# A decoder block on one core: low parts of the attention scores as pairs of 64-row products

## The chip, the core and the metric

The kernel runs on one core of a Trainium2 chip. The core has a matrix engine (TensorE, PE in the profile) that multiplies operands held in the on-chip memory SBUF and writes sums to PSUM, eight banks of 512 float32 in each of 128 partitions. VectorE (DVE), ScalarE (ACT) and GpSimd (POOL) do the elementwise work; SyncE (SP) issues most transfers between SBUF and device memory. Each engine works through its own queue in order, and semaphores hold an instruction until what it needs is done. The metric is the device time of one execution in microseconds. Before the change three runs took 1271.04, 1269.61 and 1268.10 us; the median is 1269.61.

## What is computed

One layer of a decoder block in float32, sequence 1024, width 1024. A normalised input goes through one combined projection; its parts feed a pooling mixer, a causal differential attention with four heads, and two gates. The gated sum goes through an output projection, and a gated feed-forward net follows. The change touches the attention, cut here to what matters:

```python
def block(args):
    qa, qb, start = args
    dist = (start + jnp.arange(Q_BLOCK))[:, None] - kpos[None, :]
    causal = dist >= 0
    bias = -slopes[:, None, None] * dist.astype(jnp.float32)[None]

    def probs(qq, kk):
        s = jnp.einsum('bhqd,bhkd->bhqk', qq, kk).astype(jnp.float32) * scale + bias
        s = jnp.where(causal, s, -jnp.inf)
        return jax.nn.softmax(s, axis=-1)

    a = probs(qa, k1) - lam * probs(qb, k2)
    return jnp.einsum('bhqk,bhkd->bhqd', a.astype(vh.dtype), vh)
```

Each head has two maps of scores, one from each pair of 64-wide queries and keys, and attends with the difference of their softmaxes.

## The kernel before

**Precision.** TensorE's float32r products keep fewer bits than float32. So each operand is split into a high part (the value cast to float32r) and a low part (the rest, cast too), and a product of two operands is made as three: high by high, high by low, low by high. `triple` (lines 231 to 235) issues them.

**Stages.** The queries, keys, values and gates come from a Strassen-like scheme of seven products (`seven_steps`, lines 258 to 283): each step is four triples, and the sums lie in PSUM tiles named Y, Z and X. A unit of seven steps makes two blocks of 128 output columns; the weights are converted just ahead (`weights`, `weight_operand`). The split queries and keys of a head go to device memory in `qkd` (line 292), as 128 partitions by 2 parts (high, low) by 1024 positions, with map 0 in partitions 0 to 63 and map 1 in 64 to 127. Then comes the attention, and after it the second branch, the output projection and the feed-forward net.

**Loading a head.** `load_head` (line 632) makes three operands for the scores. In `K[:, m]`, the high part of map m's keys lies in that map's 64 partitions (`hs[m]`) and its low part in the other 64. `QA[:, m]` has the high part of the queries in both halves, and `QB[:, m]` the low part in both halves. One product over 128 rows with QA is therefore high by high plus high by low, and one with QB is low by high plus low by low. `QB` is loaded by four transfers of 64 partitions. For head 0 the function is resumed in two places: QA and K are loaded before the fourth pair of gates (line 652), QB and V after the first step of the last gate unit (line 658). Heads 1 to 3 are loaded while an earlier head is worked on (lines 843 and 894).

**Scores.** `scores` (line 731) makes one row of 128 queries of one head. The row sees 128 times (qb + 1) keys; up to 512 are one block (nj = 1), more are two equal blocks (nj = 2). For each map it takes a PSUM tile of two banks (`pair`, two such tiles in all), issues the products with QA and QB for each block, and reduces on DVE: line 754 adds the distance term `negd` and finds the extreme, and line 757 takes the exponential on ACT. `transposes` and `values` follow for earlier rows. X of a running unit and the transposed heads take their PSUM tile from the same two.

**Order.** `step` (line 875) walks these generators and, by the costs that they yield (PE and DVE work in microseconds, from `map_cost` and the like), puts products of a filler between them: the rest of the last gate unit and the first branch's projection. What comes out is not yet the queue. Outside the parts under a manual schedule, a scheduler orders the instructions of every engine anew, by readiness in its own model and by free buffers, and the semaphores hold at run time. So products that stand together in a loop can stand apart in TensorE's queue.

**Buffers.** SBUF tiles of 8 KB a partition come from 16 slots (`a8`), those of 4 KB from 14 (`b4`). The slots of 4 KB also hold the converted weights (Wh, Wl), the score rows E, their transposes AT, the outputs O, the distances `negd` and the loaded gates.

Of the kernel before, what the change touches and what calls it, by code (L numbers as in the profile page):

```python
# [11 lines left out]
F32R = mybir.dt.float32r  # L12
# [3 lines left out]
P = 128  # L16
S = 1024
# [24 lines left out]
def block_kernel(ctx, tc, x, w_in, pool_mix, pool_scale, w_branch_a, lam_q1, lam_k1, lam_q2,  # L42
                 lam_k2, subln_g, w_branch_b, w_out, mix_pre_g, mix_post_g, ffn_pre_g, ffn_post_g,
                 w_ffn_gate, w_ffn_up, w_ffn_down, out):
    nc = tc.nc
    x, out = x[0], out[0]
# [16 lines left out]
    def name(s):  # L63
        uid[0] += 1
        return f"{s}_{uid[0]}"

    def a8(shape, dt, s):
        return sb.tile(shape, dt, tag="a8", bufs=A8, name=name(s))

    def b4(shape, dt, s):  # L70
        return sb.tile(shape, dt, tag="b4", bufs=B4, name=name(s))
# [7 lines left out]
    def pair(s):  # L79
        return ps.tile([P, 2, HALF], F32, tag="pair", bufs=2, name=name(s))  # L80

    def small(n, s):
        return sm.tile([P, n], F32, tag="small", bufs=20, name=name(s))

    def f32(ap):
        return ap.bitcast(F32)
# [205 lines left out]
    qkd = [[dr.tile([P, 2, S], F32, name=name("qkd")) for _ in range(2)] for _ in range(NH)]  # L292
# [318 lines left out]
    for i in range(2):  # L611
        nc.vector.tensor_tensor_reduce(out=lamt[:, 4, :], in0=lamt[:, 2 * i, :], in1=lamt[:, 2 * i + 1, :],
                                       scale=1.0, scalar=0.0, op0=ALU.mult, op1=ALU.add,
# [16 lines left out]
    hs = [slice(0, HD), slice(HD, P)]  # L630

    def load_head(h):

        QA, K = (a8([P, 2, S], F32R, n) for n in ("QA", "K"))
        for m in range(2):
            r, r2 = hs[m], hs[1 - m]
            nc.sync.dma_start(f32(K[r, m, :]), qkd[h][1][r, 0, :])
            nc.sync.dma_start(f32(K[r2, m, :]), qkd[h][1][r, 1, :])
            for rr in (r, r2):
                nc.sync.dma_start(f32(QA[rr, m, :]), qkd[h][0][r, 0, :])  # L640
        yield
        QB, V = (a8([P, 2, S], F32R, n) for n in ("QB", "V"))
        for m in range(2):
            for rr in hs:
                nc.sync.dma_start(f32(QB[rr, m, :]), qkd[h][0][hs[m], 1, :])
        nc.sync.dma_start(f32(V), vd[h])
        heads[h] = QA, QB, K, V.rearrange("p i (b d) -> p b i d", b=NB)

    head0 = load_head(0)
    for i, pair_cols in enumerate(gate_pairs[:-1]):  # L650
        if i == 3:
# [59 lines left out]
        nc.scalar.copy(ma[t][d // 4][:, d % 4, :], o)  # L711


    def map_cost(qb):
        return 0.227 * (qb + 1), 0.23 + 0.136 * (qb + 1)

    def combine_cost(qb):
        return 0.0, 0.55 + 0.136 * (qb + 1)

    def turn_cost(n):  # L720
        return 0.109 * n, 0.15 + 0.136 * n

    def value_cost(n, last):
        return 0.24 * n, 0.35 if last else 0.0

    def row_cost(qb):
        n = qb + 1
        turns = [turn_cost(min(4, n - b)) for b in range(0, n, 4)]
        return [sum(c) for c in zip(map_cost(qb), map_cost(qb), combine_cost(qb), *turns, value_cost(n, True))]

    def scores(h, qb):

        QA, QB, K, V = heads[h]
        slope = 0.25 ** (h + 1)
        L = P * (qb + 1)
        nj = 1 if L <= HALF else 2
        w = L // nj
        q = slice(qb * P, (qb + 1) * P)
        if nj == 1:
            E = b4([P, 2, HALF], F32, "E")  # L740
            E = [E[:, 0, :L], E[:, 1, :L]]
        else:
            E = [b4([P, S], F32, "E")[:, :L] for _ in range(2)]
        nm, sums = small(2, "nm"), small(2, "sums")
        dv = negd[:, S - L:S].rearrange("p (j w) -> p j w", j=nj)
        for m in range(2):
            sc = pair("s")
            for j in range(nj):
                c = slice(j * w, (j + 1) * w)
                nc.tensor.matmul(sc[:, j, :w], QA[:, m, q], K[:, m, c], start=True, stop=False)  # L750
                nc.tensor.matmul(sc[:, j, :w], QB[:, m, q], K[:, m, c], start=False, stop=True)
            e = E[m].rearrange("p (j w) -> p j w", j=nj)

            nc.vector.tensor_tensor_reduce(out=e, in0=sc[:, :nj, :w], in1=dv, scale=-slope,
                                           scalar=3.0e38, op0=ALU.add, op1=ALU.min,
                                           accum_out=nm[:, m:m + 1])
            nc.scalar.activation(E[m], E[m], AF.Exp, bias=nm[:, m:m + 1], scale=-1.0,
                                 accum_out=sums[:, m:m + 1])
            yield map_cost(qb)
        rec, cf = small(2, "rec"), small(1, "cf")  # L760
        nc.vector.reciprocal(rec, sums)
        nc.vector.tensor_scalar(cf, sums[:, 0:1], rec[:, 1:2], nlam, op0=ALU.mult, op1=ALU.mult)
        nc.vector.scalar_tensor_tensor(out=E[0], in0=E[1], scalar=cf, in1=E[0], op0=ALU.mult, op1=ALU.add)
        attends[h, qb] = E[0], rec
        yield combine_cost(qb)
# [67 lines left out]
    def filling():  # L833
        yield from last_unit
        for i in range(2):
            y2.append((a8([P, 2, S], F32R, "y2h"), a8([P, 2, S], F32R, "y2l")))
            for j in range(2):
                for t, s in zip(y2[i], range(2)):
                    nc.sync.dma_start(f32(t[:, j, :]), yd[2 * i + j][:, s, :])
        ma.extend([[a8([P, 4, HALF], F32, "ma") for _ in range(KD // 4)] for _ in range(2)])  # L840
        first = branch(0, w_branch_a, quad_mov(y2), take_a)
        next(first)
        for _ in load_head(1):
            pass
        yield from first
        next(second)
# [11 lines left out]
    AHEAD = 4  # L858
    steps, late = 0, []
    whole = [sum(c) for c in zip(*(row_cost(qb) for _, qb in seq))]  # L860
    whole[0] += FILLING * (24 + 4 * 2 * KD)
    done = [0.0, 0.0]
# [26 lines left out]
    for i in range(-AHEAD, len(seq)):  # L889
        j = i + AHEAD  # L890
        if j < len(seq):
            h, pos = divmod(j, len(QORDER))
            if pos == 2 and 0 < h < NH - 1:
                for _ in load_head(h + 1):
                    pass
            step(scores(*seq[j]))
        j = i + 1
        if 0 <= j < len(seq):
            step(transposes(*seq[j]))
        if i >= 0:  # L900
            step(values(*seq[i]))
            h, pos = divmod(i, len(QORDER))
            if h < NH - 1 and pos == len(QORDER) - 1:
                head_norm(h)
            elif h == NH - 1 and pos < NH - 1:
                for t in range(2):
                    turn_head(pos, t)
            elif h == NH - 1 and pos % 4 == 3:
                b = slice(4, 8) if pos == 3 else slice(0, 4)
                head_norm(h, b)  # L910
                defer(LAG, partial(turn_head, h, b.start // 4))
# [365 lines left out]
    for n, (i, kb) in enumerate(stream):  # L1277
        fetch(n + DEPTH + 3)
        if n + DEPTH < len(stream):
            j, kj = stream[n + DEPTH]  # L1280
# [52 lines left out]
```

## Time and profile before

| | |
|---|---|
| median of three runs | 1269.61 us |
| span of the profiled execution | 1265.6 us |
| lowest and highest run | 1268.10, 1271.04 us |
| mean granted TensorE clock | 0.998 |
| first and last start of a score product | 327.2 and 481.1 us |
| score products with QA, with QB | 96, 96 |
| transposes of the score rows (line 778), products with V (line 792) | 144, 288 |

The profile is of one execution; the span runs from its first to its last instruction. A line of groups names the source line, the engine, the operation, the tiles (out<-in), the shapes and the count, then the busy time, the mean duration in nanoseconds and the idle time ahead with what ended it. PEld is the weight load of a product, which can run under the product before it. In the timeline the first column is the start and the second the duration in microseconds; the ends of products are modelled, and they overlap. A line of windows gives the stretch and its length, then busy time and count of PE, PEld, DVE, ACT and POOL (of PE and PEld alone, where only these have work on the chosen line), the granted clock, the share of the DMA engines and GB/s. A line of waits says who waited for whom: total, times and longest, in microseconds. SPq is SyncE's queue of transfers.

### The profile page before, as it was taken

What the parts mean: (1) busy time and instruction counts of PE and PEld (TensorE: products, weight loads), DVE (VectorE), ACT (ScalarE), POOL (GpSimd) and SP (SyncE); (2) the same over time, 40 slices, a digit from 0 to 9 for tenths busy, and PEclk for the clock granted to TensorE, in tenths of its full rate; (3) what the DMA queues carried; (4) which work ended last, traced back from release to release, by engine and by line L of the source; (5) the groups of instructions that cost most, each with busy time, mean ns of one, the idle gap of its engine ahead of it and who ended that gap; (6) DMA issues with size and microseconds to landing.
All of it is one profiled execution on the core that took longest, in us unless ns stands there. A gap on an engine that the chain in (4) does not pass through costs nothing.

```text
span 1265.6 us, 15699 instructions
## 1 busy us (share of the span) xinstructions
PE 1246.5 (98%) x5912; PEld 1039.1 (82%) x5912; DVE 838.6 (66%) x1296; ACT 582.7 (46%) x1042; POOL 142.7 (11%) x128
## 2 busy tenths in 40 slices
PE   8999999999999999999999999999999999999997
PEld 7888888888788887888888888888888888888886
DVE  5985784534578888855697655655656547955666
ACT  7553344434477774444553333333333333554542
POOL 4100000000201100000102111011111011000221
PEclk9999999999999999999999999999999999999999
DMA  7354338323797108533314322323322368733236
GB/s 253 114 189 132 135 128 243 115 85 117 259 250 206 34 18 283 169 115 134 117 45 139 125 100 89 103 100 108 125 99 84 125 215 279 238 95 105 87 96 208
DMA packets 135452, 179.15 MB, mean 142 GB/s; under 512 B 7632, under 2 KB 90320, under 8 KB 132944
## 3 DMA queue, kind: packets, MB, share of 16 engines
q1 hardware_dynamic: 124544, 146.56, 37.0%
q10 hardware_dynamic: 10832, 31.59, 6.5%
q8 instruction: 46, 0.75, 0.3%
q14 instruction: 30, 0.25, 0.1%
HBM read 124.39 MB, written 53.74 MB: 141 GB/s over the span
## 4 chain that ended last, share of the span: by engine, by line
PE 89%; DVE 3%; ACT 2%; DMA 2%; issue 2%; POOL 1%; SPq 0%; POOLq 0%; DVEq 0%; ACTq 0%
PE Y L235 10%; PE Y L234 10%; PE Y L233 10%; PE X L235 5%; PE X L234 5%; PE X L233 5%; PE Z L235 3%; PE Z L234 3%; PE Z L233 3%; PE Yd L234 3%; PE Yd L235 3%; PE Yd L233 3%; PE o L792 2%; PE branch L233 2%; PE branch L235 2%; PE branch L234 2%
## 5 line engine op out<-in xcount | busy, mean ns | idle before, releaser
L162 DVE TENSOR_TENSOR p<-Z,p 128x512 f32<-128x512 f32 x35 | 24.2, 691 | 163.3 <-PE Z L235 160.7
L234 PE MATMUL Y<-A_lo,Wh 128*128 128x512 f32 x296 | 115.5, 390 | 0.3 <-DVE A_lo L89 0.3
L233 PE MATMUL Y<-A_hi,Wh 128*128 128x512 f32 x296 | 115.2, 389 | 0.0
L235 PE MATMUL Y<-A_hi,Wl 128*128 128x512 f32 x296 | 115.2, 389 | 0.0
L233 PE MATMUL Y<-S_hi,Wh 128*128 128x512 f32 x280 | 109.2, 390 | 0.0
L233 PE MATMUL X<-S_hi,Wh 128*128 128x512 f32 x280 | 109.2, 390 | 0.0
L235 PE MATMUL Y<-S_hi,Wl 128*128 128x512 f32 x280 | 109.1, 390 | 0.0
L234 PE MATMUL Y<-S_lo,Wh 128*128 128x512 f32 x280 | 109.1, 390 | 0.0
L235 PE MATMUL X<-S_hi,Wl 128*128 128x512 f32 x280 | 108.9, 389 | 0.0
L234 PE MATMUL X<-S_lo,Wh 128*128 128x512 f32 x280 | 108.9, 389 | 0.0
L202 ACT CAST Wh<-wf_t 128x1024 fp32r<-128x1024 f32 x70 | 72.8, 1053 | 72.1 <-PE X L234 30.6
L202 ACT CAST Wh<-w_raw 128x1024 fp32r<-128x1024 f32 x72 | 60.6, 843 | 66.7 <-PE Z L234 40.0
L89 DVE TENSOR_TENSOR w_op<-wd,w_op 128x512 fp32r<-128x512 f32 x77 | 56.1, 729 | 52.8 <-ACT w_op L166 52.6
L89 DVE TENSOR_TENSOR Wl<-wf_t,Wh 128x1024 fp32r<-128x1024 f32 x70 | 86.6, 1245 | 4.8 <-ACT Wh L202 4.8
L166 ACT CAST w_op<-wd 128x512 fp32r<-128x512 f32 x77 | 47.9, 622 | 78.1 <-PE Yd L235 31.4
L89 DVE TENSOR_TENSOR Wl<-w_raw,Wh 128x1024 fp32r<-128x1024 f32 x72 | 70.4, 977 | 14.5 <-ACT Wh L202 14.5
L233 PE MATMUL Yd<-w_op,s_op 128*128 128x512 f32 x176 | 68.7, 390 | 0.6 <-ACT w_op L166 0.6
L234 PE MATMUL Yd<-w_op,s_op 128*128 128x512 f32 x176 | 68.7, 390 | 0.3 <-DVE w_op L89 0.3
L235 PE MATMUL Yd<-w_op,s_op 128*128 128x512 f32 x176 | 68.3, 389 | 0.0
L162 DVE TENSOR_TENSOR wf_t<-w_raw,wf_t 128x512 f32<-128x512 f32 x70 | 65.7, 938 | 1.1
L234 PEld LDWEIGHTS Y<-A_lo,Wh 128*128 128x128 f32 x296 | 55.6, 188 | 12.1 <-DVE A_lo L89 0.7
L233 PEld LDWEIGHTS Y<-A_hi,Wh 128*128 128x128 f32 x296 | 55.6, 188 | 11.6
(269 smaller groups left out, 3058.7 us busy)
## 6 DMA issues: line engine op xcount, KB each, us to landing
s_raw<-fsd SPq DMA_DIRECT2D x35, 512.0 KB, 3.6
w_raw<-in_w_in_dram SPq DMA_DIRECT2D x32, 512.0 KB, 4.3
w_raw<-in_w_ffn_gate_dram SPq DMA_DIRECT2D x22, 512.0 KB, 3.8
w_raw<-in_w_ffn_up_dram SPq DMA_DIRECT2D x22, 512.0 KB, 3.8
fsd<-fss SPq DMA_DIRECT2D x11, 1024.0 KB, 3.9
wd<-in_w_ffn_down_dram SPq DMA_DIRECT2D x44, 256.0 KB, 5.4
fsd<-F SPq DMA_DIRECT2D x33, 256.0 KB, 2.3
qkd<-qk_st ACTq DMA_DIRECT2D x16, 512.0 KB, 3.8
```

The lines of the kernel that those rows point to most:

```text
L89: nc.vector.tensor_tensor(out=o, in0=a, in1=f32(hi), op=ALU.subtract)
L162: nc.vector.tensor_tensor(out=o, in0=a, in1=b, op=op)
L166: nc.scalar.copy(hi, a)
L202: nc.scalar.copy(hi, a)
L233: nc.tensor.matmul(o, ah, bh, start=start, stop=False, skip_group_check=goes_on)
L234: nc.tensor.matmul(o, ah, bl, start=False, stop=False, skip_group_check=goes_on)
L235: nc.tensor.matmul(o, al, bh, start=False, stop=stop, skip_group_check=goes_on)
L792: nc.tensor.matmul(o, ats[b // 4][:, j, b % 4 * P:(b % 4 + 1) * P], V[:, b, :, :], start=b == 0 and j == 0, stop=b == qb and j == 1)
```

## The change

`QB` becomes one tile of 4 KB that holds the low part of the queries as it lies in device memory, map 0 in partitions 0 to 63 and map 1 in 64 to 127, and is loaded by one transfer, ahead of the point where `load_head` is left for the first time. `scores` takes the PSUM tiles of both maps at once and issues the products with QA for map 0, then for map 1. Then, block by block, it issues for each map a product over the 64 partitions of that map, on `QB[hs[m]]` and the high part of the keys. The built program marks these with a division of the array into 64 rows by 128 columns, at row 0 for map 0 and at row 64 for map 1. The term low by low is no longer computed. The reductions follow after all products of both maps. The planner's costs change with it: the PE cost of a row's two maps, twice 0.227 for each block of 128 keys, becomes 0.34, all put down to the first.

```diff
@@ load_head
+        QB = b4([P, S], F32R, "QB")
+        nc.sync.dma_start(f32(QB), qkd[h][0][:, 1, :])
         yield
-        QB, V = (a8([P, 2, S], F32R, n) for n in ("QB", "V"))
-        for m in range(2):
-            for rr in hs:
-                nc.sync.dma_start(f32(QB[rr, m, :]), qkd[h][0][hs[m], 1, :])
+        V = a8([P, 2, S], F32R, "V")
         nc.sync.dma_start(f32(V), vd[h])
@@ costs
-    def map_cost(qb):
-        return 0.227 * (qb + 1), 0.23 + 0.136 * (qb + 1)
+    def map_cost(qb, m):
+        return (0.34 * (qb + 1), 0.0)[m], 0.23 + 0.136 * (qb + 1)
...
@@ scores
+        sc = [pair("s") for _ in range(2)]
         for m in range(2):
-            sc = pair("s")
             for j in range(nj):
-                c = slice(j * w, (j + 1) * w)
-                nc.tensor.matmul(sc[:, j, :w], QA[:, m, q], K[:, m, c], start=True, stop=False)
-                nc.tensor.matmul(sc[:, j, :w], QB[:, m, q], K[:, m, c], start=False, stop=True)
+                nc.tensor.matmul(sc[m][:, j, :w], QA[:, m, q], K[:, m, j * w:(j + 1) * w], start=True, stop=False)
+        for j in range(nj):
+            for m in range(2):
+                nc.tensor.matmul(sc[m][:, j, :w], QB[hs[m], q], K[hs[m], m, j * w:(j + 1) * w],
+                                 start=False, stop=True)
+        for m in range(2):
             e = E[m].rearrange("p (j w) -> p j w", j=nj)
 
-            nc.vector.tensor_tensor_reduce(out=e, in0=sc[:, :nj, :w], in1=dv, scale=-slope,
+            nc.vector.tensor_tensor_reduce(out=e, in0=sc[m][:, :nj, :w], in1=dv, scale=-slope,
                                            scalar=3.0e38, op0=ALU.add, op1=ALU.min,
                                            accum_out=nm[:, m:m + 1])
             nc.scalar.activation(E[m], E[m], AF.Exp, bias=nm[:, m:m + 1], scale=-1.0,
                                  accum_out=sums[:, m:m + 1])
-            yield map_cost(qb)
+            yield map_cost(qb, m)
```

In the changed program the products with QA stand on line 748 and those with QB on line 751.

More of the change, by code (lines that the diff above doesn't have):

```diff
@@ L728, in row_cost @@
         turns = [turn_cost(min(4, n - b)) for b in range(0, n, 4)]
-        return [sum(c) for c in zip(map_cost(qb), map_cost(qb), combine_cost(qb), *turns, value_cost(n, True))]
+        return [sum(c) for c in zip(map_cost(qb, 0), map_cost(qb, 1), combine_cost(qb), *turns, value_cost(n, True))]
     def scores(h, qb):
```

## The prediction

> **What bounds the kernel now.** I read the page first (busy time, chain of waits), then the windows of the stage that the change touches, then that stage's waits, then single products in the timeline.
>
> ```profile
> span 1265.6 us, 15699 instructions
> PE 1246.5 (98%) x5912; PEld 1039.1 (82%) x5912; DVE 838.6 (66%) x1296; ACT 582.7 (46%) x1042; POOL 142.7 (11%) x128
> ...
> PE 89%; DVE 3%; ACT 2%; DMA 2%; issue 2%; POOL 1%; SPq 0%; POOLq 0%; DVEq 0%; ACTq 0%
> ```
>
> TensorE is busy for 98% of the span and carries 89% of the chain that ended last. The scores run from 327 to 481 us. The windows give the whole stage (span, then PE, weight loads, DVE, ACT, POOL), and the products of lines 751 and 750 alone:
>
> ```profile
> 325.00:482.00 157.00, 154.07 (x910) 132.28 (x908) 124.90 (x311) 111.11 (x289) 17.36 (x9) 1.00 0.53 158
> ...
> 325.00:482.00 157.00, 32.75 (x96) 18.11 (x96) 1.00 0.53 158
> ...
> 325.00:482.00 157.00, 33.65 (x96) 18.09 (x96) 1.00 0.53 158
> ```
>
> Here, too, TensorE has 3 us of idle time in 157, and its clock is granted in full (1.00). DVE at 125 us and ACT at 111 us leave room. So what is added to TensorE's queue lengthens the kernel, and what is taken out shortens it. TensorE's waits in this stage are few:
>
> ```profile
> PE s L751 <- DMA QB<-qkd: 1.9, 1, 1.9
> PE oT L826 <- DVE O L811: 1.2, 1, 1.2
> PE o L792 <- DVE O L798: 0.8, 2, 0.6
> PE s L750 <- DVE nm L754: 0.7, 3, 0.3
> ```
>
> What one product costs is read from starts that follow each other, since the durations overlap (column 1 is the start, column 2 the duration):
>
> ```profile
> 440.05 0.39 PE L751 MATMUL s<-K,QB 128*128 128x512 f32 x1
> 440.28 0.39 PE L750 MATMUL s<-K,QA 128*128 128x512 f32 x1
> ...
> 446.19 0.36 PE L751 MATMUL s<-K,QB 128*128 128x448 f32 x1
> 446.39 0.36 PE L750 MATMUL s<-K,QA 128*128 128x448 f32 x1
> ...
> 450.41 0.35 PE L751 MATMUL s<-K,QB 128*128 128x384 f32 x1
> 450.59 0.34 PE L750 MATMUL s<-K,QA 128*128 128x384 f32 x1
> ```
>
> A low product takes 0.23 us at 512 columns, 0.20 at 448 and 0.18 at 384. It is recorded for 0.39 us, so 0.16 us of it is still in flight while the next product streams.
>
> **The change, part by part.** *The low products themselves.* The 96 low products stay 96, over the same columns; each now uses 64 rows of the array in place of 128. One that stands alone streams the same columns and saves nothing. Time falls only where a product in rows 0 to 63 is followed directly by one in rows 64 to 127, so that both stream at once. Whether it is depends on the order of TensorE's queue, which the scheduler makes and not the loops. In the built program it is this for the third and fourth row of queries ("..." stands for products of the running unit and transposes):
>
> ```
> L748 Matmult s_2830<-K_2143,QA_2142 128x448 x2
> L751 Matmult s_2830<-K_2143,QB_2152 128x448 x2
> ...
> L748 Matmult s_2831<-K_2143,QA_2142 128x448 x2
> L751 Matmult s_2831<-K_2143,QB_2152 128x448 x2
> ...
> L748 Matmult s_2863<-K_2143,QA_2142 128x256
> L751 Matmult s_2863<-K_2143,QB_2152 128x256
> ...
> L748 Matmult s_2864<-K_2143,QA_2142 128x256
> L751 Matmult s_2864<-K_2143,QB_2152 128x256
> ```
>
> The second map's products come later, with other work between; I take the reason to be its score buffer, which comes free later. I counted through the whole queue: the 96 low products stand in 66 groups, and only 9 of the 48 possible pairs are neighbours, 3 of 512 columns, 2 of 448 and 4 of 384. If these overlap fully they save 3 x 0.23 + 2 x 0.20 + 4 x 0.18 = 1.8 us; if not, nothing. I take 1.8.
>
> *The switches.* Each of the 66 groups is entered from a product over all 128 rows and left to one: 132 changes between the whole array and half of it. The trace of before has no 64-row product, so the price has to be bounded. From below: nothing. Products of other lines, shapes and buffers follow each other at the same 0.23 us now, and a change of rows could be just as free. For the upper end, two things that are hidden now could be laid open. One is the 0.16 us in flight, if the array must be empty before its division changes. The other is the weight load:
>
> ```profile
> 334.47 0.47 PE L751 MATMUL s<-K,QB 128*128 128x512 f32 x1 [1.85 <-DMA QB<-qkd]
> 334.78 0.40 PE L750 MATMUL s<-K,QA 128*128 128x512 f32 x1
> 335.01 0.39 PE L751 MATMUL s<-K,QB 128*128 128x512 f32 x1
> ...
> 334.55 0.19 PEld L750 LDWEIGHTS s<-K,QA 128*128 128x128 f32 x1
> 334.78 0.19 PEld L751 LDWEIGHTS s<-K,QB 128*128 128x128 f32 x1
> ...
> 448.99 0.71 PE L778 MATMUL aT<-ident,E 128*128 128x128 f32 x5
> 449.45 0.48 PE L233 MATMUL branch<-y2h,wb_hi 128*128 128x512 f32 x1
> 449.77 0.39 PE L234 MATMUL branch<-y2l,wb_hi 128*128 128x512 f32 x1
> ```
>
> In the steady run a load (0.19 us) starts with the product before it (334.78 beside 334.78) and costs nothing. Where it could not, after the wait at 334.47 and after the short transposes at 448.99, the next start comes 0.31 and 0.32 us later in place of 0.23: an uncovered load costs 0.09. So a switch lies between 0 and 0.16 + 0.09 = 0.25 us, and 132 of them between 0 and 33 us. The two nearest rows are the uncovered load (0.09) and the tail (0.16); I know of no row that tells which one a switch lays open, and take their middle, 0.125 us: 16.5 us. TensorE has no idle time near the groups that would hide it.
>
> The Trainium skill, in "TensorEngine Tiling (Array Packing)", Key Properties, says that changing the tiling mode drains TensorE, whereas a change of tile within one mode does not. The 0.39 against 0.23 us above is what such a drain would expose; no row here shows one. By that rule alone the term would be 132 x 0.16 = 21 us in place of 16.5. The same skill, in "TensorE: Matmul & The Clock Gate", Part 3, has products on different row groups start about 4 ns apart; this agrees with full overlap of the nine pairs and changes nothing in the sum.
>
> *The load of QB.* The four 64-row loads of a head become one of 128 rows, half the bytes, into a 4 KB tile. For head 0 it moves up in SP's queue from behind the weights of the last unit to between those of the gate units. Now it is late:
>
> ```profile
> 328.75 2.54 SPq L645 DMA_DIRECT2D QB<-qkd  x4
> ...
> 332.23 0.39 PE L235 MATMUL Y<-S_hi,Wl 128*128 128x512 f32 x1
> ```
>
> The last lands just before 334.47, and TensorE stands for 1.85 us (row above). The new place is several units of some 20 us earlier, so this wait goes: 1.85 us saved. What is late next? Both maps of the first row now stand together at 327.5 and take both score buffers, and X of the running unit needs one of them. The first reduction needs the distances:
>
> ```profile
> 329.28 1.04 POOL L664 TENSOR_SCALAR_AFFINE_SELECT negd<-negd 128x1024 f32<-128x1024 f32 x1
> ...
> L754 DVE CUSTOM_DVE_ANT_0 E<-s,negd 128x1024 f32<-128x1024 f32 x8 | 9.7, 1218 | 10.7 <-PE s L751 10.7
> ```
>
> It ends no earlier than 329.28 + 1.04 + 1.22 = 331.5 us. The built queue has 15 products of Z and Y (15 x 0.23 = 3.4 us) between the scores, done at about 329.3, and X: covered to 332.7. Without that cover it would cost 2.2 us.
>
> *The 4 KB slot and the order.* QB now holds one of 14 slots of 4 KB for a head's length, and two while heads overlap, and gives back one of 16 of 8 KB. In the gate units the slots hold converted weights; their casts wait for TensorE to free them (40.0 us behind Z), not the other way round:
>
> ```profile
> L202 ACT CAST Wh<-w_raw 128x1024 fp32r<-128x1024 f32 x72 | 60.6, 843 | 66.7 <-PE Z L234 40.0
> L89 DVE TENSOR_TENSOR Wl<-w_raw,Wh 128x1024 fp32r<-128x1024 f32 x72 | 70.4, 977 | 14.5 <-ACT Wh L202 14.5
> ```
>
> A cast and its subtraction (0.84 + 0.98 us) lie beside twelve products (2.7 us), so one slot less costs nothing; were the cover gone, 1.8 us in each of four units, 7 us. For heads 1 to 3 QB moves behind V on SP, and head 3's also behind two weight loads of the second branch; the scores that need it come later in TensorE's queue. Nothing, unless the slot comes late (a rival). The new costs of the planner only deal the same filler products differently between the rows: nothing, within the 0.7 us of waits for DVE shown above.
>
> *Sum:* 16.5 - 1.8 - 1.85 = +12.9 us on the span of 1265.6, so 1278.5. The median of the runs, 1269.6, lies 4.0 above that span; with these the time is 1282.5.
>
> **The rivals.** (1) *Faster: a switch is free.* From 0.028 us a switch (3.65 / 132) the balance turns. If changing rows is no more than a change of line, what is left is the wait for QB and nine overlapped pairs: 1269.6 - 3.7 = 1266. For it: no handover now shows a gap of its own, apart from uncovered loads. Against: all of these handovers leave the array whole. (2) *The dear switch:* tail and load are both laid open, 33.0 - 3.7 = +29.3, 1299. For it: a load for another division may have to wait for the drain too. Against: nothing shows that loads for the two divisions exclude each other. (3) *The change doesn't do what it says:* the pairs hardly ever meet, nothing overlaps, and switches are free: the 1.85 us alone, 1267.8. (4) *QB comes late in heads 1 to 3:* its slot is granted late, SP holds it in order, and the head's first low product stands.
>
> ```profile
> SPq L645 <- PE s L751: 8.7, 1, 8.7
> ...
> 329.42 4.92 DMA QB<-qkd
> ```
>
> Today QB's load waited once for 8.7 us for a slot, with no harm to TensorE. If three heads each stood for the 4.9 us that the loads of head 0 took to land, that is 15 us, 1269.6 + 15 - 3.7 = 1281, even with free switches.
>
> **How the numbers follow.** Forecast (a switch between 0.05 and 0.2 us) 0.42; dear switch 0.18; late QB 0.06; free switch 0.22; nothing but QB's wait 0.12. A measurement of this kernel tells 0.2%, 2.5 us, from no change. Faster is the free switch: 0.22. Same is the third rival: 0.12. Slower is the rest: 0.66. The range goes from the free switch with one microsecond of order (1265) to the dear one with the same (1300). The forecast's own range is 132 x 0.05 - 3.7 = +3 to 132 x 0.2 - 3.7 = +23: 1273 to 1292.
>
> **What would show it.** Right: starts of a lone 64-row product and of the product behind it are 0.1 us or more further apart than 0.23 (0.20, 0.18), with TensorE counted busy or idle and nothing named as releaser; the two of a neighbouring pair start within a few hundredths; no wait for QB near 334; the score stage is longer by some 13 us and all others are unchanged. Wrong: the steps around low products are as before, and the time is at or below 1268; or low products wait for DMA or for DVE, so that order and slots decide and not switches; or the stretch outside the scores moves.

## The result, and the profile after

The changed kernel takes 1285.96 us (median of four runs, 1285.63 to 1289.29) against 1270.3 for the kernel before beside it: a ratio of 1.0134, 95% interval 1.0121 to 1.0148. The change makes the kernel slower by 1.3%. The forecast was 1282.5, its range 1265 to 1300.

The span grew from 1265.6 to 1284.1 us, by 18.5, and TensorE's busy time by 19.6. From the page of the kernel after:

```profile
span 1284.1 us, 15691 instructions
PE 1266.1 (99%) x5912; PEld 1037.1 (81%) x5912; DVE 838.6 (65%) x1296; ACT 583.4 (45%) x1042; POOL 144.0 (11%) x128
```

The windows of three stages, of the kernel before and then of the one after (stretch, length, busy time and count of PE, PEld, DVE, ACT, POOL, then clock, DMA share, GB/s):

```profile
0.00:327.00 327.00, 321.18 (x1566) 270.23 (x1567) 203.86 (x279) 153.35 (x224) 23.77 (x38) 1.00 0.46 149
327.00:482.00 155.00, 152.07 (x901) 130.61 (x899) 123.78 (x310) 109.93 (x287) 15.36 (x9) 1.00 0.53 155
482.00:1265.00 783.00, 773.27 (x3449) 638.21 (x3447) 510.96 (x709) 319.45 (x531) 103.60 (x82) 1.00 0.41 136
```

```profile
0.00:327.00 327.00, 320.89 (x1566) 269.81 (x1567) 204.08 (x279) 153.24 (x224) 23.73 (x38) 1.00 0.46 151
327.00:500.00 173.00, 171.14 (x895) 128.48 (x894) 125.13 (x309) 110.59 (x287) 15.40 (x9) 1.00 0.43 127
500.00:1284.00 784.00, 774.09 (x3454) 638.83 (x3453) 509.36 (x710) 319.60 (x531) 104.87 (x82) 1.00 0.41 135
```

The score stage alone grew, from 155 to 173 us. In it TensorE is busier than before (idle 1.9 us in place of 2.9), and DVE and ACT do the same work. So the 18 us are neither waits for other engines nor for transfers: they lie between one TensorE product and the next. The timeline of the kernel after shows a lone 64-row product (column 1 is the start, column 2 the duration):

```profile
358.20 0.34 PE L748 MATMUL s<-K,QA 128*128 128x384 f32 x1
...
358.46 0.18 PEld L751 LDWEIGHTS s<-K,QB 64*128 64x128 f32 x1 [0.19 <-issue]
358.46 0.43 PE L751 MATMUL s<-K,QB 64*128 64x384 f32 x1
358.83 0.19 PEld L233 LDWEIGHTS branch<-y2h,wb_hi 128*128 128x128 f32 x1 [0.18 <-issue]
358.83 0.50 PE L233 MATMUL branch<-y2h,wb_hi 128*128 128x512 f32 x1
358.94 0.19 PEld L234 LDWEIGHTS branch<-y2l,wb_hi 128*128 128x128 f32 x1
359.16 0.39 PE L234 MATMUL branch<-y2l,wb_hi 128*128 128x512 f32 x1
```

Read the starts against the steps of before (0.18 us for 384 columns, 0.23 for 512). From QA's product to the low one it is 0.26, from there to the next 0.37, and from that to the one behind it 0.33: 0.08, 0.19 and 0.10 too much, 0.37 us in all. The two load rows show where it goes. In the steady run a load starts with the product before its own. Here it starts with its own product, at 358.46 and again at 358.83, and the profile names nothing that it waited for ("issue"). So each switch first holds the next load back for about 0.09 us, and then the load itself lies open for about 0.10. The 0.08 is the hold of the first switch, the 0.19 the load of the first and the hold of the second, the 0.10 the load of the second. I read the hold as the emptying of the array and call it that below. The trace doesn't show it empty: at all 132 switches the next product starts 0.07 us ahead of the recorded end of the one before, and these ends are modelled.

This is so at all places. The medians of the steps over the stage: the product before a switch takes 0.326 us at 512 columns (13 of them) and 0.268 at 384 (13), a lone 64-row product 0.426 (12) and 0.370 (10), the product of 512 columns behind a switch back 0.337 (39). Against 0.231 and 0.175, the plain steps (medians between products over all rows), that is 0.09, 0.195 and 0.106 too much.

Where two 64-row products on the two halves of the array are neighbours, they overlap. The first row of queries, in the kernel after and then in the run with all rows (below), which has the same order there:

```profile
327.52 1.07 PE L748 MATMUL s<-K,QA 128*128 128x512 f32 x4
328.52 0.73 PE L751 MATMUL s<-K,QB 64*128 64x512 f32 x4
329.19 0.50 PE L233 MATMUL Z<-A_hi,Wh 128*128 128x512 f32 x1
329.52 0.39 PE L234 MATMUL Z<-A_lo,Wh 128*128 128x512 f32 x1
```

```profile
327.29 1.07 PE L748 MATMUL s<-K,QA 128*128 128x512 f32 x4
328.19 1.07 PE L751 MATMUL s<-K,QB 128*128 128x512 f32 x4
329.10 0.39 PE L233 MATMUL Z<-A_hi,Wh 128*128 128x512 f32 x1
329.33 0.39 PE L234 MATMUL Z<-A_lo,Wh 128*128 128x512 f32 x1
```

Four low products take 0.67 us (328.52 to 329.19) in place of 0.91, even with a load and an emptying among them. But QA's four take 1.00 in place of 0.90, and the product behind takes 0.33 in place of 0.23. In this group, the one with the most columns in the queue, the gain is 0.04 us.

### The profile page after: what moved, and what is told of

It reads as the page before. It is cut to its first block, busy times and chain, and to the rows that moved or that the text cites. A ratio compares the mean times of both kernels' runs of the same rounds, so it can differ in the third digit from the quotient of the medians.

```text
span 1284.1 us, 15691 instructions
## 1 busy us (share of the span) xinstructions
PE 1266.1 (99%) x5912; PEld 1037.1 (81%) x5912; DVE 838.6 (65%) x1296; ACT 583.4 (45%) x1042; POOL 144.0 (11%) x128
## 5 line engine op out<-in xcount | busy, mean ns | idle before, releaser
L166 ACT CAST w_op<-wd 128x512 fp32r<-128x512 f32 x77 | 47.8, 621 | 70.9 <-PE Yd L235 31.8
L235 PEld LDWEIGHTS Y<-A_hi,Wl 128*128 128x128 f32 x296 | 55.6, 188 | 11.7 <-issue 0.2
```

The source lines that it names most:

```text
L166: nc.scalar.copy(hi, a)
L235: nc.tensor.matmul(o, al, bh, start=False, stop=stop, skip_group_check=goes_on)
```

## The experiments

Three theories. S: the switches cost, about 0.2 us each, two for a group of 64-row products. O: the new order costs, with both maps' score buffers taken at once and QB in a slot of 4 KB. R: a 64-row product is slow by itself, wherever it stands. Each run is timed beside the kernel before.

### All rows, nothing else undone

```diff
-                nc.tensor.matmul(sc[m][:, j, :w], QB[hs[m], q], K[hs[m], m, j * w:(j + 1) * w],
+                nc.tensor.matmul(sc[m][:, j, :w], QB[:, q], K[:, m, j * w:(j + 1) * w],
                                  start=False, stop=True)
```

> The change, but each low product runs over all 128 rows: QB (4 KB, both maps' low parts) against the whole of K[:, m], so that rows of the other map add its low queries times the low part of this map's keys, a term of the size of the one that the change leaves out. Loads, loops, buffers and planner costs are those of the change; no division of the array is left. Theory S (each of the 66 groups of 64-row products pays about 0.39 us for its two switches, 25.7 us in all, and 9 neighbouring pairs give 1.8 back): 1286.0 - 25.7 + 1.8 = 1262, with the waits that 3 us more or less of order bring, 1260 to 1267, below the time of before. Rival O (the new order, with both maps' score buffers taken at once, and the 4 KB slot make the stage longer): the order is nearly the same, so 1283 to 1287. Rival R (a 64-row product is slow by itself, 0.2 us each of 96): 1286 - 19 = 1267.

Measured: 1266.45 us, ratio to before 0.9977 (0.9966 to 0.9988). The whole loss goes with the division of the array; what remains of the change is a small gain. O falls: loops, buffers and slot are those of the change. R stands as yet, with 1267. The windows of this run's stage:

```profile
327.00:481.00 154.00, 151.72 (x898) 130.45 (x898) 123.75 (x310) 109.26 (x287) 15.66 (x9) 1.00 0.47 143
```

### One map in 64 rows

```diff
             for m in range(2):
-                nc.tensor.matmul(sc[m][:, j, :w], QB[hs[m], q], K[hs[m], m, j * w:(j + 1) * w],
+                r = hs[0] if m == 0 else slice(0, P)
+                nc.tensor.matmul(sc[m][:, j, :w], QB[r, q], K[r, m, j * w:(j + 1) * w],
```

> The change, but only map 0's low products use 64 rows; map 1's run over all 128 (low queries of both maps against K[:, 1], as in the run with all rows). In the built queue the 48 64-row products stand in 38 groups and no pair is left. S: 38 x 0.39 = 14.8 us above the version without any division, 1262 + 15 = 1277 (1274 to 1281). O: 1283 to 1287. R: 48 x 0.2 = 9.6 above it, 1272 if that version is at 1262.

Measured: 1278.64 us, ratio 1.0074 (1.005 to 1.0097): 12.2 us above all rows, 0.32 for each of the 38 groups. S had 1274 to 1281. R had 1272, but on a base of 1262; on the measured 1266.45 it would be 1276.0 and S 1281.3, so the time alone doesn't tell them apart. A group of two low products, which stand in the same half, does:

```profile
369.17 0.63 PE L748 MATMUL s<-K,QA 128*128 128x512 f32 x2
369.73 0.73 PE L752 MATMUL s<-K,QB 64*128 64x512 f32 x2
370.39 0.50 PE L235 MATMUL branch<-y2h,wb_lo 128*128 128x512 f32 x1
```

The two take 0.66 us, 0.20 above two plain steps; if each were slow by 0.2 itself, it would be 0.40. The step of the first is 0.340 us and that of the second 0.319 (512 columns, medians of two each), 0.109 and 0.088 too much: the open load behind the one switch and the hold of the next, now seen apart.

### Every 64-row product alone

```diff
-        sc = [pair("s") for _ in range(2)]
         for m in range(2):
+            sc = pair("s")
             for j in range(nj):
-                nc.tensor.matmul(sc[m][:, j, :w], QA[:, m, q], K[:, m, j * w:(j + 1) * w], start=True, stop=False)
-        for j in range(nj):
-            for m in range(2):
-                nc.tensor.matmul(sc[m][:, j, :w], QB[hs[m], q], K[hs[m], m, j * w:(j + 1) * w],
-                                 start=False, stop=True)
-        for m in range(2):
+                c = slice(j * w, (j + 1) * w)
+                nc.tensor.matmul(sc[:, j, :w], QA[:, m, q], K[:, m, c], start=True, stop=False)
+                nc.tensor.matmul(sc[:, j, :w], QB[hs[m], q], K[hs[m], m, c], start=False, stop=True)
...
-        return (0.34 * (qb + 1), 0.0)[m], 0.23 + 0.136 * (qb + 1)
+        return 0.227 * (qb + 1), 0.23 + 0.136 * (qb + 1)
```

> The 64-row low products and the 4 KB QB of the change, but in the loops and with the planner costs of before: per map and block the product with QA, then the one with QB. In the built queue all 96 low products stand alone, each between products over 128 rows: 96 groups, no pair. S: 96 x 0.39 = 37 us above the version without division, 1299 to 1306: slower than the change by 13 to 20 us. O: the old order is back, so close to before, 1267 to 1271. R: 96 x 0.2 = 19 us above that version, 1283 to 1287, as the change.

Measured: 1298.94 us, ratio 1.0241 (1.0207 to 1.0275): 32.5 us above all rows, 0.34 for each of the 96 groups. It has as many 64-row products as the change and is 13 us slower, so R falls; and it has the loops of before, so O falls once more. From its timeline, two low products close together, each with a switch on both sides:

```profile
403.40 0.34 PE L749 MATMUL s<-K,QA 128*128 128x384 f32 x1
403.66 0.44 PE L750 MATMUL s<-K,QB 64*128 64x384 f32 x1
404.03 0.50 PE L234 MATMUL branch<-y2l,wb_hi 128*128 128x512 f32 x1
404.37 0.34 PE L749 MATMUL s<-K,QA 128*128 128x384 f32 x1
404.64 0.44 PE L750 MATMUL s<-K,QB 64*128 64x384 f32 x1
405.01 0.66 PE L777 MATMUL aT<-ident,E 128*128 128x128 f32 x4
```

QA's product takes 0.26 and 0.27, the low one 0.37 both times: the steps of the change.

### All pairs neighbours, by a critical section

```diff
-        for j in range(nj):
+        with tc.tile_critical():
+          for j in range(nj):
             for m in range(2):
                 nc.tensor.matmul(sc[m][:, j, :w], QB[hs[m], q], K[hs[m], m, j * w:(j + 1) * w],
```

> The change, with each row's low products kept together in TensorE's queue (a critical section around their loops): 32 groups, and all 48 pairs are neighbours. S: 32 x 0.39 = 12.5 us for switches, 8.6 us saved by overlap (12 x 0.231 + 8 x 0.203 + 12 x 0.175 + 8 x 0.147 + 4 x 0.120 + 4 x 0.108), so 4 us above the version without division: 1264 to 1270, no gain over before worth the name. O: the stage is bound by order, and tighter grouping makes it no better: 1284 to 1290. R: overlap halves the cost, 96 products in 48 slots: about 1262 + 10 - 9 = 1263.

Measured: 1327.75 us, ratio 1.0461 (1.0436 to 1.0487), far outside all three. The score tiles' view shows what ended TensorE's and its loads' idle time, the waits name what TensorE's low products stood for (two of the lines), and the windows show the stage:

```profile
  PEq L749: 48.8, 21
```

```profile
PE s L752 <- DMA y2h<-yd: 6.6, 1, 6.6
...
PE s L752 <- ACT O L800: 4.5, 8, 1.2
```

```profile
327.00:400.00 73.00, 54.56 (x246) 40.57 (x244) 29.75 (x71) 27.44 (x64) 7.82 (x5) 0.88 0.71 203
...
327.00:540.00 213.00, 172.37 (x893) 130.29 (x891) 125.77 (x306) 108.23 (x285) 15.12 (x9) 0.91 0.36 102
```

Of 213 us TensorE is idle for 41: it waits at the entry of the section (line 749), in part for work that its products don't use (y2h and O are no operands of line 752), and its mean granted clock is 0.91 here. The run tells what the section costs and nothing on the switches, so adjacency was tried again without it.

### All pairs neighbours, by order alone

```diff
-                nc.tensor.matmul(sc[m][:, j, :w], QA[:, m, q], K[:, m, j * w:(j + 1) * w], start=True, stop=False)
+                last = nc.tensor.matmul(sc[m][:, j, :w], QA[:, m, q], K[:, m, j * w:(j + 1) * w],
+                                        start=True, stop=False)
         for j in range(nj):
             for m in range(2):
-                nc.tensor.matmul(sc[m][:, j, :w], QB[hs[m], q], K[hs[m], m, j * w:(j + 1) * w],
-                                 start=False, stop=True)
+                with tc.issue_after(last.ins), tc.high_priority():
+                    last = nc.tensor.matmul(sc[m][:, j, :w], QB[hs[m], q], K[hs[m], m, j * w:(j + 1) * w],
+                                            start=False, stop=True)
```

> The change, with the low products of a row queued directly behind each other and behind both maps' products with QA, by edges of order and priority and without a critical section: 32 groups, all 48 pairs neighbours. Where the adjacency run spent its time was waiting at the critical section and not on TensorE's work, so that wait is not expected here. S, with the 0.33 us a group that the runs with 38 and 96 groups gave: 32 x 0.33 = 10.6, less 8.6 for overlap, on the 1266.5 of all rows: 1268 to 1273, with some us more if the scores, which now come later against the filler, run out of cover at the end. If adjacency itself is what costs: 1285 and more.

Measured: 1272.11 us, ratio 1.0022 (1.0004 to 1.004). A second run leaves the priority out:

> As the run before, without the priority: 43 groups, 42 of the 48 pairs neighbours. S: 43 x 0.33 = 14.2 less 7.5 for overlap, on 1266.5: 1271 to 1276. If adjacency itself is what costs: between the change and the critical section.

Measured: 1275.92 us, ratio 1.006 (1.0043 to 1.0077). Both lie where S puts them and far below the change, so adjacency helps. But even with all 48 pairs the switches take more than the overlap gives: 5.7 us above all rows. From the timeline and the windows of the run with priority:

```profile
353.08 0.51 PE L748 MATMUL s<-K,QA 128*128 128x384 f32 x2
353.52 0.62 PE L753 MATMUL s<-K,QB 64*128 64x384 f32 x4
354.07 0.66 PE L782 MATMUL aT<-ident,E 128*128 128x128 f32 x4
```

```profile
327.00:486.00 159.00, 155.69 (x893) 122.43 (x891) 123.17 (x306) 107.80 (x285) 15.27 (x9) 0.99 0.46 137
```

Four low products of 384 columns take 0.55 us where four steps of 0.175 would be 0.70. With overlap counted (8.6 us for the 48 pairs, each taken at the plain step of its columns, and 7.4 for the 42), a group costs (5.7 + 8.6) / 32 = 0.45 us here, and (9.5 + 7.4) / 43 = 0.39 in the run without priority, more than the 0.33 of the groups that stand apart. The switch is no dearer here: what exceeds the plain step around 64-row products adds up to 3.2 us in the trace of the run with priority, which makes (3.2 + 8.6) / 32 = 0.37 for a group. Elsewhere in the stage it is 8.3 us, against 6.4 with all rows, so the rest lies in other waits and open loads; TensorE's idle time is 3.3 us against 2.3.

### The loops of before with the new load

The edit is that of the lone products, with all rows of QB and K in the low product.

> The 4 KB QB and its early single load, over all 128 rows, but in the loops and with the planner costs of before: per map and block the product with QA, then the one with QB. No division of the array. Against before only the load and its slot differ. The wait for QB (1.85 us) is gone: 1.85 below before. If the short waits for score buffers that the loops of both maps did without (17 loads that waited for DVE, 5.4 us of load time, about 2 us of TensorE's) come back, the time lies 2 us above the run with all rows in the new loops; if the slot of 4 KB costs, at or above before.

Measured: 1266.89 us, ratio 0.9984 (0.9974 to 0.9993). Below before by 2.3 us, and not to be told from the new loops (1266.45): the new load is a gain, and taking both score buffers at once is neither gain nor loss that these runs can see.

### QB late again

```diff
-        QB = b4([P, S], F32R, "QB")
-        nc.sync.dma_start(f32(QB), qkd[h][0][:, 1, :])
         yield
+        QB = b4([P, S], F32R, "QB")
+        nc.sync.dma_start(f32(QB), qkd[h][0][:, 1, :])
```

> The run with all rows in the new loops, but with QB loaded behind the point where the loading function is left, as before, still by one transfer and into 4 KB. The first low product stands in the queue where QB is late: if the early load is worth what the wait showed, 1.85 us above the run with all rows. The scheduler puts other products ahead of it, so it may be less: 0 to 2 us.

Measured: 1272.97 us, ratio 1.0032 (1.0019 to 1.0045): 6.5 us above all rows, where 0 to 2 was expected. The wait is there, in the waits of the stage:

```profile
PE s L751 <- DMA QB<-qkd: 2.5, 1, 2.5
PE aT L780 <- DVE O L800: 1.7, 1, 1.7
```

This is not quite the load of before: in SyncE's queue QB now stands behind V, and the low product that waits starts at 336.52 us, where it was 334.47. The profiled span is 3.8 us above that with all rows (1268.2 against 1264.4): 2.5 is this wait, and 1.3 the second line, which is 0.4 with all rows. But the profiled execution, at 1270.0 us, is the lowest of ten runs that go up to 1277.41. Over these the time goes with the mean granted clock, from 0.998 at 1270.0 to 0.993 at 1277.41, and 0.5% of 1270 us is about 6 us. The ten runs with all rows are all at 0.998 to 1.0, and the kernel before, whose QB is late too, has a run of 1276.52 at 0.993. Why a late QB and a lower clock come together was not looked at.

### The planner's old costs

```diff
-        return (0.34 * (qb + 1), 0.0)[m], 0.23 + 0.136 * (qb + 1)
+        return 0.227 * (qb + 1), 0.23 + 0.136 * (qb + 1)
```

> The run with all rows in the new loops (both maps at once, 4 KB QB loaded early), with the planner's PE cost of before (0.227 for each map and block of keys), which fits products over all rows better than 0.34 for both maps. It is meant as the version that keeps what the change gains and pays no switch. If the filler's place matters little, as the prediction took it: the same as with all rows, 1265 to 1268, 0.2% below before. If the changed costs were a loss of their own: lower still, by 1 us or more.

Measured: 1266.12 us, ratio 0.998 (0.997 to 0.9991), as with the new costs. This version and the one with all rows are faster than both kernels: they keep the single early load of half the bytes and give up the division. In place of the term that the change leaves out, their low products add one of its size that doesn't belong there: the other map's low queries times the low part of this map's keys.

### The runs together

| version | groups of 64 rows | neighbouring pairs | us | above all rows | for a group |
|---|---|---|---|---|---|
| all rows | 0 | 0 | 1266.45 | | |
| one map | 38 | 0 | 1278.64 | 12.2 | 0.32 |
| the change | 66 | 9 | 1285.96 | 19.5 | (19.5 + 1.8) / 66 = 0.32 |
| every product alone | 96 | 0 | 1298.94 | 32.5 | 0.34 |

The time follows the number of groups, not that of 64-row products (48, 96 and 96). The change was timed apart from the rest, beside runs of the kernel before at 1270.3 us in place of 1268.86; measured against these it has 0.30 for a group. The steps of the trace give 0.37 to 0.39. That the runs give less has a reason in the traces: added over all steps of the stage, what exceeds the plain step is 22.7 us around 64-row products in the change and 2.9 elsewhere, against 6.4 with all rows. The balance, 22.7 + 2.9 - 6.4 = 19.2, is near the 19.5 of the runs; with every product alone it is 36.6 + 1.6 - 6.4 = 31.8 beside 32.5. So in the change some 3.5 us that the stage loses elsewhere with all rows are gone. I take it that these open loads and short waits now fall together with a switch.

## Why the prediction came out as it did

**TensorE's queue bounds the stage.** Right: the stage grew by 18 us with TensorE busy throughout, and the stages ahead of it and behind it are the same (327 and 327, 783 and 784 us).

**The pairs.** Right: nine neighbouring pairs, which overlap (the two starts lie 3 to 4 ns apart in the trace); the run in which all pairs are neighbours is 13.9 us faster than the change.

**The switches.** The mechanism was right and the size was off. This is the mis-sized term: 132 switches at 0.125 us, 16.5 us, taken as the middle between an open load (0.09) and the 0.16 us that a product is in flight. The prediction set these against each other, and the dear switch, with both laid open, was a rival. Both are laid open. The load costs 0.10, near its row; the emptying costs 0.09, not the whole 0.16. That makes 0.19 us a switch by the steps, and net by the runs (19.5 + 1.8) / 132 = 0.16: 21.3 us in place of 16.5. The error was to take a middle of two costs that can fall together, without a reason that only one of them does.

The rule of the Trainium skill, in "TensorEngine Tiling (Array Packing)", Key Properties, that a change of tiling mode drains TensorE, agrees with the trace: every start behind a switch comes late and nothing is named as releaser, though the draining itself is not seen. The hold measures 0.09 us, and the uncovered load comes on top of it. That the 21.3 us lie near the 21 which the prediction gives for this rule alone is luck: those were 0.16 us of draining and no load. The 4 ns that the Trainium skill gives between products on different row groups, in "TensorE: Matmul & The Clock Gate", Part 3, agree with the 3 to 4 ns between the two starts of a pair in the run with all pairs neighbours.

**QB's load.** Right: the wait near 334 us is gone. TensorE's longest waits in the stage are now two for DVE, as the kernel after shows:

```profile
PE aT L780 <- DVE O L800: 1.0, 1, 1.0
PE oT L828 <- DVE O L813: 0.9, 1, 0.9
```

The loops of before with the new load are 2.3 us below before, where 1.85 was said; with the late load the wait is back.

**Order and slot.** Right that they cost nothing. X of the running unit was said to be covered until 332.7 us, and it starts at 332.73:

```profile
332.50 0.39 PE L235 MATMUL Y<-S_hi,Wl 128*128 128x512 f32 x1
332.73 0.39 PE L233 MATMUL X<-S_hi,Wh 128*128 128x512 f32 x1
```

The rival of a late QB in heads 1 to 3 did not come: no wait for it stands in the stage's waits. The new planner costs change nothing, as the last run shows.

**The sum.** Forecast +12.9 us; measured +18.5 on the span and +15.7 between the medians of the runs beside each other. The 4.0 us between span and median of before were added as fixed. After the change it is 1285.96 - 1284.1 = 1.9, and with all rows 1266.45 - 1264.4 = 2.1; every run's time lies 1.7 to 2.0 us above its own span. So some 2 of the 4.0 us were chance of the profiled execution. That the time missed by 3.5 us and the span by 5.6 is luck of this kind: it hid 2 us of the missing switch cost.

## What to carry to other kernels

Price a division of the array by the number of changes between divisions in the built queue, not by the products that use it: here a change costs 0.16 to 0.19 us, so two of them take more than a pair of 512 columns saves (0.23), and a group must hold two pairs of 512 columns to come out about even. Count neighbours in the queue after scheduling; a loop that writes two products side by side does not place them so. And when a change loses, look for the part that gains: here the one early load of half the bytes was worth 0.2% and needed no division.

## What had not been expected

With a critical section around TensorE's low products, TensorE was idle for 41 of 213 us, and its mean granted clock was 0.91 in the stage (0.88 in its first 73 us, where TensorE was idle for 18). One wait of 2.5 us for QB, put back alone, raised the median by 6.5 us and spread the runs from 1270.0 to 1277.4; 1.3 us went into a second wait, and the slower runs had the lower clock, but what ties the clock to the late load is open.
